# Sums of squares through PSUM on VectorE alone, and a place of its own for the last phase's scaled x, in a planned decoder-layer kernel

## The chip, the cores and the metric

The kernel runs on one core of one Trainium2 chip. The metric is the time of one execution on the device in microseconds (us); the number before is the median of three runs. The engines are named as the profile names them: PE (TensorE, matrix products; PEld is its loading of weights), DVE (VectorE), ACT (ScalarE), POOL (GpSimd) and SP (SyncE, which starts most transfers). SBUF is the working memory that all engines read and write; PSUM holds what PE produces, in eight banks, and DVE and ACT can read and write it.

## The reference

One layer of a hybrid decoder for two groups of requests: a prompt of 1024 tokens, and eight samples of one token each with a cache of 512 tokens. The width is 1024, the inner width of the two feed-forward networks 2816. Cut to what matters here:

```python
def rmsnorm(x, g):
    y = xf * lax.rsqrt(jnp.mean(xf * xf, axis=-1, keepdims=True) + NORM_EPS)
    return (y * g).astype(x.dtype)

def decoder_layer(...):
    h = x + 0.5 * rmsnorm(swiglu(rmsnorm(x, n_ffn1_pre), ffn1_gate, ffn1_up, ffn1_down), n_ffn1_post)
    u = rmsnorm(h, n_mix_pre)
    proj = u @ w_in
    ...                       # differential attention and RWKV-7 time mixing of proj
    h = h + rmsnorm(concat(ya, yb) @ w_out, n_mix_post)
    h = h + 0.5 * rmsnorm(swiglu(rmsnorm(h, n_ffn2_pre), ffn2_gate, ffn2_up, ffn2_down), n_ffn2_post)
```

So each feed-forward network has a norm in front of it and one behind it, and the mixing has one in front and one behind. Each norm needs the mean of the squares of a token's 1024 values.

## The kernel before

**Layout.** Activations lie transposed: the 1024 features are 8 tiles of 128 partitions, the tokens run along the free dimension. The tokens are cut into two halves of 512 (the eight samples ride with the first half of each feed-forward network, which makes 520), and each half into two chunks of about 260 (`CHUNKS`, line 33). The full precision of float32 is kept by splitting each operand of a large product into a high and a low part of type float32r and forming three products (`mm3`, line 678). The split of an activation is made by `pair` (line 808): ACT writes the high part with the norm's gain, DVE subtracts it again and writes the low part.

**Phases.** The trunk (`s_trunk`, line 1016) runs the feed-forward networks in four phases: ph 0 and 1 are the first network on the two halves of the tokens, ph 2 and 3 the second network. Phases 0 and 3 save products by a seven-product scheme on blocks (`seven`, `s_combine`); phase 3 builds those blocks in the SBUF region with the tag `dreg`. In between, while the trunk goes on, run the input projection (`s_project`, tiles `proj_m`), the jobs of the RWKV part (`s_job`, tiles `job_*`), attention (`s_attend`), the samples' own decode (`s_decode_a`, `s_decode_b`, tiles `dec_*` and `decb_*`), and the output projection (`s_out`, tiles `out_m` and `outb_m`).

**Where norms are formed.** `square_sum` (line 755) squares one of the 8 feature tiles on ACT and adds it to a sum; `rstd` (line 765) adds over the partitions with one matmul against a matrix of 1/1024, then takes the square root on ACT and the reciprocal on DVE. `stats` (line 799) does both for all 8 tiles of a chunk. It is called in two places:

- `s_stats` (line 1206), ahead of phases 2 and 3, with one buffer `sqs` for the squares (in the trace `stats_sqs`), the sum in the tile `bset_bv`;
- `s_tail` (line 1242), behind phases 0 and 1, for the norm ahead of the projection, with the two buffers `sq` (in the trace `tail_sq`), the sum in `init_rb` (the name `prb` in the code). The projection is run on the values without this norm, and its result is multiplied with it as it leaves PSUM (`init_E<-proj_m,init_rb`).

The sums over the down product's results (`trunk_acc` with `trunk_sq`) and over the output projection's results (`bset_la`, `bset_sg` with `init_E`) call `square_sum` directly.

With `SQP` at 0 the add goes to whichever of DVE and POOL `choose` (line 431) expects to end first. `s_pre` (line 1214) prepares x of a phase: scale with the norm, then `pair`. In phase 3 the scaled value goes into a ring of two buffers `sq` (in the trace `pre_sq`), which the block combination, the down sums and others use too; in phases 1 and 2 it overwrites its source. The split parts `pre_T` of phase 3 take the buffers that the operands of the second output projection (`outb_T`) occupied.

**Order.** Nothing is left to the order of the source. Each part is a generator of instructions, a stream, and a planner written in Python (`run`, line 478) picks at every step, for each engine, among the streams' next instructions the one with the earliest due time that can start soon. Costs come from `price` (line 380). The due times come from a backward pass over a dry run (`latest`, line 567); `PASSES` dry runs follow each other, each with the due times of the one before, and `BIAS` adds a number of microseconds to all due times of a stream (`tail1` is the second stream of the name `tail`, and so on). The chosen order is then fixed for each engine. An engine executes its own queue strictly in that order, and PE is such a queue too.

PSUM banks are handed out by name. A stream outside the trunk has one or a few: `stats`, `pre`, `lora`, `job`, `outn` and `decb` all have `dec`; a tail of phase 0 or 1 has `dec` and `aux0` in turn, where the norm of the tail's first chunk lies in `aux0` and that of its second in `aux1`. A new tile in a bank waits until the former one has been read.

Of the kernel before, what the change touches and what calls it, by code (L numbers as in the profile page):

```python
# [22 lines left out]
P = 128  # L23
# [56 lines left out]
W_DEC = 4160  # L80
# [9 lines left out]
MW = 1  # L90
MARG = 0
SLACK = 0.02
PASSES = 4
BIAS = {"trunk2": 300, "outn3": -60, "outb0": 30, "pre2": -3, "tail1": -30, "lora1": -10}
SHIFT = {}
SWAP = 0
MIX = 1
SQP = 0
RESAT = 3
GROUPS = {(0, 10): [[0, 1, 2], [3, 4], [5, 6, 7], [8, 9]], (3, 6): [[0, 1, 2], [3], [4, 5]],  # L100
          (0, 8): [[0, 1, 2], [3, 4], [5], [6, 7]], (0, 6): [[0, 1, 2], [3], [4, 5]], (3, 4): [[0, 1], [2, 3]], (3, 8): [[0, 1, 2], [3, 4], [5], [6, 7]]}
LOWS = (1, "out")
# [110 lines left out]
class Kern:  # L213
# [99 lines left out]
    def put(self, eng, op, fn, a, k):  # L313
# [14 lines left out]
        if o.late is not None:  # L328
            o.late += BIAS.get(st.part, 0) + sum(d for a, b, d in self.shift.get(st.part, ()) if a <= o.key[1] < b)
        self.price(o, op, a, k, outs[0], ins)  # L330
# [468 lines left out]
    def stats(self, src, rb, tmp=("sqs", 1), **kw):  # L799

        for k in range(KT):
            if SQP:
                self.square_sum(rb, src[k], k, self.ps2()[:, :rb.shape[-1]], engines=("vector",))
            else:
                self.square_sum(rb, src[k], k, self.tmp(*tmp, rb.shape[-1]), **kw)
        self.rstd(rb)
# [407 lines left out]
    def s_pre(self, ph):  # L1214

        half = ph % 2
        if ph > 1:
            yield ("wait", ("outw", half))
        for c, (_, n) in enumerate(CHUNKS[ph]):
            yield ("wait", ("stage", ph, c))  # L1220
            if ph:
                yield ("wait", ("stats", ph, c))
            if c == 0:
                tiles = self.two(half)
                x = self.x[ph] = self.parts(ph, *tiles)
                self.xt[ph] = [t.rearrange("p (k t) -> p k t", t=520) for t in tiles]
            for k in range(KT):
                src = self.staged[c]
                if ph:

                    t = self.tmp("sq", 2, n) if ph == 3 else src[k]
                    self.either("tensor_tensor", t, src[k], self.own[c][2][:, :n], ALU.mult)
                    src = {k: t}
                for step in self.pair(k, src, f"n_ffn{1 + ph // 2}_pre", x[c]):
                    step()
                if k % 4 == 3:
                    yield
            self.signal(("x", ph, c))
            yield
        self.signal(("staged", ph))  # L1240
# [205 lines left out]
    def s_project(self, half):  # L1446

        nc = self.nc
        places = None
        for c in range(2):  # L1450
            yield ("wait", ("prb", half, c))
        if half:
            yield ("wait", ("outw", 0))
        else:
            yield ("wait", ("loaded", 1, "up", LEAD - 1, None))
            places = ("w0", "w1"), [("used", 1, kind, LEAD - 1, None) for kind in ("gate", "up")]

        job = [16, 12, 20]
        ms = [24, 25] + job
        ms = ms + [m + i for i in range(1, 4) for m in job] + list(range(12)) if half else \  # L1460
            ms + [m + 1 for m in job] + list(range(8)) + [m + i for i in range(2, 4) for m in job] + list(range(8, 12))

        def out(i, c, ps):
            o, n = SPANS[half][c]
            po = (self.rb if i % 2 else self.E)[:, o:o + n]
            nc.vector.tensor_tensor(po, ps, self.prb[:, o:o + n], ALU.mult)
            nc.sync.dma_start(self.PT[ms[i]][:, FIRST[half] + o:FIRST[half] + o + n], po)
            if c:
                self.signal(("done", half, ms[i]))

        units = [(i, c) for i in range(len(ms)) for c in ((2,) if half and i > 1 else range(2))]
        if half:
            units[:4] = [(0, 0), (1, 0), (0, 1), (1, 1)]
        yield from self.linear(("in", half), [self.column(self.I["w_in"], m) for m in ms], units, None, out, places,
                               [(self.Li[m], half == 0) for m in ms] if "in" in LOWS else None)
        self.signal(f"proj{half}")

    def s_out(self, half):
# [1169 lines left out]
```

## Time and profile before

| what | value |
|---|---|
| runs shown | 2285.0, 2285.44 and 2281.86 us, median 2285.0 |
| the profiled execution's own time | 2287.04 us |
| its span, first to last instruction | 2284.6 us |
| granted clock of TensorE, mean | 0.995 |
| PE busy | 2223.3 us, 15857 matmuls |
| DVE, ACT, POOL busy | 1537.3, 1098.8 and 986.9 us |
| transfers | 343.15 MB, 150 GB/s in the mean |

How to read the rows that follow in the prediction. A row of a group or of a tile names the engine, the operation, what it writes and reads (`out<-in`, by the program's names), the shapes and the count; then the shortest, the median and the longest duration in ns with the first and last start in us, or the sum in us and the mean in ns, with the idle time in front. A row of the timeline begins with its start and duration in us, and what stands in brackets is the idle time of the engine before it and what ended that. A row of waits names who waited for whom, with the total in us, the count and the longest. Nearly every operation carries the line L320, since all are recorded by one helper; the tile's names tell them apart.

### The profile page before, as it was taken

What the parts mean: (1) busy time and instruction counts of PE and PEld (TensorE: products, weight loads), DVE (VectorE), ACT (ScalarE), POOL (GpSimd) and SP (SyncE); (2) the same over time, 40 slices, a digit from 0 to 9 for tenths busy, and PEclk for the clock granted to TensorE, in tenths of its full rate; (3) what the DMA queues carried; (4) which work ended last, traced back from release to release, by engine and by line L of the source; (5) the groups of instructions that cost most, each with busy time, mean ns of one, the idle gap of its engine ahead of it and who ended that gap; (6) DMA issues with size and microseconds to landing.
All of it is one profiled execution on the core that took longest, in us unless ns stands there. A gap on an engine that the chain in (4) does not pass through costs nothing.

```text
span 2284.6 us, 42790 instructions
## 1 busy us (share of the span) xinstructions
PE 2223.3 (97%) x15857; PEld 1981.1 (87%) x15857; DVE 1537.3 (67%) x3550; ACT 1098.8 (48%) x2256; POOL 986.9 (43%) x819
## 2 busy tenths in 40 slices
PE   7999999999999999999999999999999998999998
PEld 7999999799887778888877877777788888999998
DVE  5477888745766776568766466664676365778776
ACT  5443443635454366344562155543576555544444
POOL 3344555524333675456443124333434354544443
PEclk9999999999999999999999999999999999999999
DMA  6423334354433685655668753334636857434543
GB/s 203 135 84 94 110 93 131 102 148 140 113 107 104 184 244 174 211 177 151 178 205 213 193 146 111 106 86 115 199 112 172 276 165 240 148 114 126 148 139 112
DMA packets 476295, 343.15 MB, mean 150 GB/s; under 512 B 82457, under 2 KB 424061, under 8 KB 476088
## 3 DMA queue, kind: packets, MB, share of 16 engines
q1 hardware_dynamic: 475480, 338.82, 50.6%
q8 instruction: 125, 2.05, 0.4%
q0 software_dynamic: 320, 1.08, 0.1%
q14 instruction: 82, 0.67, 0.1%
q10 hardware_dynamic: 288, 0.52, 0.1%
HBM read 278.98 MB, written 61.38 MB: 149 GB/s over the span
## 4 chain that ended last, share of the span: by engine, by line
PE 77%; DVE 6%; ACT 6%; DMA 5%; issue 3%; POOL 2%; SPq 1%; DVEq 0%; ACTq 0%; POOLq 0%
PE trunk_m L320 44%; PE proj_m L320 12%; PE trunk_aux L320 7%; PE job_aux L320 4%; PE out_m L320 2%; PE outb_m L320 2%; PE attn_m L320 2%; PE attn_aux L320 1%; SPq L320 1%; ACT wts_w L320 1%; ACT mix_T L320 1%; DMA wts_raw<-in_ffn_gate_dram 1%; PE job_dec L320 1%; DMA lin_w<-Lo 1%; POOL wts_w L320 1%
## 5 line engine op out<-in xcount | busy, mean ns | idle before, releaser
L320 POOL TENSOR_TENSOR wts_w<-wts_raw,wts_w 128x1024 fp32r<-128x1024 f32 (+2 forms) x161 | 310.8, 1938 | 351.3 <-ACT wts_w L320 303.5
L320 PE MATMUL trunk_m<-trunk_xl,wts_w 128*128 128x256 f32 (+2 forms) x2700 | 456.5, 320 | 4.4 <-DVE trunk_xl L320 3.7
L320 PE MATMUL trunk_m<-pre_X,wts_w 128*128 128x512 f32 (+3 forms) x2400 | 439.9, 334 | 4.9 <-DVE pre_X L320 2.0
L320 PEld LDWEIGHTS trunk_m<-trunk_xl,wts_w 128*128 128x128 f32 x2700 | 381.4, 188 | 40.7 <-DVE trunk_xl L320 5.8
L320 PEld LDWEIGHTS trunk_m<-pre_X,wts_w 128*128 128x128 f32 x2400 | 351.3, 190 | 44.8 <-issue 3.7
L320 PE MATMUL trunk_m<-pre_T,wts_w 128*128 128x512 f32 (+3 forms) x1848 | 365.0, 348 | 6.5 <-DVE trunk_xl L320 2.7
L320 ACT CAST wts_w<-wts_raw 128x1024 fp32r<-128x1024 f32 (+2 forms) x293 | 244.2, 848 | 241.3 <-PE trunk_m L320 167.2
L320 PEld LDWEIGHTS trunk_m<-pre_T,wts_w 128*128 128x128 f32 x1848 | 288.1, 191 | 44.3 <-issue 3.9
L320 DVE TENSOR_TENSOR trunk_xl<-trunk_xl,trunk_m 128x256 f32<-128x256 f32 (+2 forms) x351 | 165.9, 491 | 57.7 <-PE trunk_m L320 56.4
L320 POOL TENSOR_TENSOR trunk_xl<-trunk_t,trunk_xl 128x512 fp32r<-128x512 f32 (+3 forms) x88 | 94.7, 1078 | 169.2 <-ACT trunk_xl L320 168.8
L320 PE MATMUL proj_m<-tail_xl,lin_w 128*128 128x256 f32 (+1 forms) x1248 | 166.5, 288 | 0.0
L320 PEld LDWEIGHTS proj_m<-tail_xl,lin_w 128*128 128x128 f32 x1248 | 153.9, 188 | 6.9 <-issue 5.1
L320 PE MATMUL proj_m<-tail_T,lin_w 128*128 128x512 f32 (+1 forms) x672 | 150.4, 380 | 3.0 <-DVE tail_T L320 1.9
L320 PEld LDWEIGHTS proj_m<-tail_T,lin_w 128*128 128x128 f32 x672 | 120.6, 188 | 31.0 <-DVE tail_T L320 3.0
L320 DVE TENSOR_TENSOR wts_w<-wts_raw,wts_w 128x1024 fp32r<-128x1024 f32 (+2 forms) x102 | 109.6, 1075 | 34.7 <-ACT wts_w L320 32.4
L320 POOL TENSOR_TENSOR lin_w<-lin_raw,lin_w 128x1024 fp32r<-128x1024 f32 x21 | 51.6, 2457 | 110.6 <-ACT lin_w L320 106.7
L320 ACT CAST wts_w<-wts_lraw 128x512 fp32r<-128x512 f32 x94 | 55.7, 619 | 72.0 <-DMA wts_lraw<-in_ffn_down_dram 35.0
L320 POOL TENSOR_TENSOR wts_w<-wts_lraw,wts_w 128x512 fp32r<-128x512 f32 x43 | 60.0, 1398 | 45.2 <-ACT wts_w L320 41.9
L320 PE MATMUL trunk_aux<-trunk_xl,wts_w 128*128 128x256 f32 (+1 forms) x516 | 71.7, 283 | 0.0
L320 DVE TENSOR_TENSOR trunk_t<-trunk_g,trunk_m 128x512 f32<-128x512 f32 (+2 forms) x75 | 41.9, 559 | 44.1 <-PE trunk_m L320 41.7
L320 PE MATMUL trunk_m<-comb_T,wts_w 128*128 128x260 f32 x540 | 69.4, 282 | 0.0
L320 ACT CAST wts_w<-wts_dec 128x512 fp32r<-128x512 f32 x30 | 17.6, 587 | 103.7 <-DVE wts_dec L320 102.0
(647 smaller groups left out, 4263.8 us busy)
## 6 DMA issues: line engine op xcount, KB each, us to landing
wts_raw<-in_ffn_gate_dram SPq DMA_DIRECT2D x88, 512.0 KB
wts_raw<-in_ffn_up_dram SPq DMA_DIRECT2D x58, 512.0 KB
wts_raw<-in_ffn_down_dram SPq DMA_DIRECT2D x56, 384.0 KB
wts_raw<-in_ffn_down_dram SPq DMA_DIRECT2D x29, 512.0 KB
lin_raw<-in_w_in_dram SPq DMA_DIRECT2D x26, 512.0 KB
wts_w<-Ld SPq DMA_DIRECT2D x22, 512.0 KB
mix_T<-PT SPq DMA_DIRECT2D x37, 256.0 KB
Ld<-wts_w SPq DMA_DIRECT2D x24, 384.0 KB
```

Source lines behind the costliest of these rows:

```text
L320: o = Op(eng, lambda: fn(*a, **k), st)
```

## The change

Three things are edited, beside one switch without effect (`ODD = 0` leaves the line in `s_project` as it was).

1. `SQP` names the two kinds of buffers for which `stats` now puts the square of each feature tile into a PSUM bank of the stream (`ps2`) instead of an SBUF buffer, and gives the add to DVE alone. Both callers of `stats` are named, so it holds for the norms ahead of phases 2 and 3 (from the bank `dec`) and for those behind phases 0 and 1 (from `dec` and `aux0` in turn). The sums over the down product and over the output projection keep their SBUF buffers and their choice of engine.
2. In phase 3 `s_pre` takes the region `dreg` as a place for all 16 scaled tiles of x, where it had the ring of two buffers `sq`.
3. The planner makes three passes instead of four, and other streams have other biases.

```diff
-PASSES = 4
-BIAS = {"trunk2": 300, "outn3": -60, "outb0": 30, "pre2": -3, "tail1": -30, "lora1": -10}
+PASSES = 3
+BIAS = {"trunk2": 300, "outn3": -50, "outb0": 90, "pre2": -3, "prep1": 3, "job11": 3, "job12": 30, "states0": -3, "lora0": 10, "lin1": -3, "stats0": -30, "mix0": -30, "stats2": -60, "decb0": 30, "attn01": -3, "stats1": 30, "fin0": -60}
...
-SQP = 0
+SQP = ("sqs", "sq")
+ODD = 0
...
     def stats(self, src, rb, tmp=("sqs", 1), **kw):
         for k in range(KT):
-            if SQP:
+            if SQP and tmp[0] in SQP:
                 self.square_sum(rb, src[k], k, self.ps2()[:, :rb.shape[-1]], engines=("vector",))
             else:
                 self.square_sum(rb, src[k], k, self.tmp(*tmp, rb.shape[-1]), **kw)
...
+                scaled = self.T(self.pool, [P, W_DEC], "dreg") if ph == 3 else None
             for k in range(KT):
                 src = self.staged[c]
                 if ph:
-                    t = self.tmp("sq", 2, n) if ph == 3 else src[k]
+                    t = scaled[:, 2112 * c + n * k:2112 * c + n * k + n] if ph == 3 else src[k]
                     self.either("tensor_tensor", t, src[k], self.own[c][2][:, :n], ALU.mult)
...
-                               [(self.Li[m], half == 0) for m in ms] if "in" in LOWS else None)
+                               [(self.Li[m], half == 0) if not ODD or m % 2 else () for m in ms] if "in" in LOWS else None)
```

## The prediction

> **What bounds the kernel now.** First I read the top of the page, for the engine that is never free.
>
> ```profile
> span 2284.6 us, 42790 instructions
> PE 2223.3 (97%) x15857; PEld 1981.1 (87%) x15857; DVE 1537.3 (67%) x3550; ACT 1098.8 (48%) x2256; POOL 986.9 (43%) x819
> ```
>
> TensorE (PE) is busy for 2223.3 of 2284.6 us, and the change touches no matmul of the weights. So all that can be won or lost is PE's idle time, 61.3 us, plus what a lower granted clock adds after a pause. Next I read the table of stages, to see where that idle time lies. Its columns are the stretch, its length, then PE, PEld, DVE, ACT and POOL busy, then the granted clock and the DMA share.
>
> ```profile
> 0.00:40.00 40.00, 28.21 (x175) 25.88 (x176) 21.36 (x56) 22.98 (x44) 15.30 (x17) 0.91 0.46 136
> 395.00:460.00 65.00, 59.84 (x323) 51.22 (x322) 45.73 (x77) 39.30 (x72) 35.56 (x39) 0.95 0.33 100
> 540.00:1000.00 460.00, 454.34 (x3336) 386.26 (x3336) 311.43 (x881) 219.37 (x498) 216.25 (x156) 1.00 0.53 158
> 1000.00:1120.00 120.00, 119.81 (x626) 101.62 (x625) 97.38 (x190) 51.84 (x85) 70.27 (x56) 1.00 0.55 162
> 1120.00:1190.00 70.00, 63.77 (x394) 56.48 (x394) 53.72 (x94) 45.29 (x80) 33.94 (x39) 0.98 0.72 217
> 1146.00:1160.00 14.00, 10.41 (x68) 9.61 (x66) 10.13 (x22) 9.87 (x18) 6.64 (x10) 0.88 0.18 51
> 1320.00:1770.00 450.00, 439.05 (x2936) 347.61 (x2935) 290.96 (x838) 251.19 (x587) 169.18 (x111) 1.00 0.47 132
> 1770.00:1905.00 135.00, 128.97 (x862) 116.36 (x861) 68.34 (x114) 74.53 (x133) 56.90 (x61) 1.00 0.68 210
> 1905.00:1960.00 55.00, 51.04 (x412) 50.63 (x411) 31.59 (x63) 32.86 (x63) 25.55 (x33) 0.97 0.91 278
> 2260.00:2284.60 24.60, 16.69 (x141) 15.81 (x139) 13.68 (x29) 15.11 (x36) 10.42 (x14) 0.95 0.23 87
> ```
>
> Length minus PE busy is the idle time: 11.8 us at the start and 7.9 us at the end, which no edit here reaches; 5.2 us around the tail of phase 0 (395 to 460); 6.2 us around the tail of phase 1 (1120 to 1190); 10.0 us around the hand-over to the last phase (6.0 and 4.0); and 5.7 and 11.0 us in the two stretches of jobs and attention. The moved norms lie at the tails (ph 0 and 1) and ahead of phases 2 and 3.
>
> **The change part by part.** *Part 1, squares to PSUM, sums on DVE.* There are four norms of two chunks with seven added squares each, 56 adds. These rows say who does them now.
>
> ```profile
> L320 POOL TENSOR_TENSOR init_rb<-init_rb,tail_sq x23: 737/754/1666, 427.4 to 1178.8; 128x256 f32<-128x256 f32 x16, 128x264 f32<-128x264 f32 x7
> L320 DVE TENSOR_TENSOR init_rb<-init_rb,tail_sq x5: 411/425/427, 438.1 to 1178.2; 128x256 f32<-128x256 f32 x5
> L320 DVE TENSOR_TENSOR bset_bv<-bset_bv,stats_sqs x16: 410/431/2385, 1011.9 to 1875.5; 128x256 f32<-128x256 f32 x12, 128x264 f32<-128x264 f32 x4
> L320 POOL TENSOR_TENSOR bset_bv<-bset_bv,stats_sqs x12: 734/770/1729, 1015.3 to 1873.1; 128x256 f32<-128x256 f32 x9, 128x264 f32<-128x264 f32 x3
> L320 DVE TENSOR_TENSOR trunk_xl<-trunk_xl,trunk_m 128x256 f32<-128x256 f32 x142 | 58.4, 414 | 14.5 <-PE trunk_m L320 14.1
> L320 ACT ACTIVATE job_dec<-mix_T,setup_rmu 128x512 f32<-128x512 f32 x24 | 16.6, 690 | 24.0 <-DMA mix_T<-PT 9.5 <-DVE job_stf L320 5.3 <-issue 3.5
> L320 ACT ACTIVATE mix_T<-mix_T,setup_cols 128x512 f32<-128x512 f32 x8 | 5.7, 716 | 0.0
> ```
>
> POOL does 23 + 12 = 35 adds at about 0.76 us and loses 27 us of work; DVE gains 35 adds. A DVE add with one operand in PSUM is in the trace (trunk_xl, 414 ns), so DVE gains at least 35 x 0.414 = 14.5 us over the whole span, at 67% busy. A Square of ScalarE (ACT) written to PSUM is not in the trace. Its bounds come from the two scaling activations of 512 columns: 690 ns into PSUM against 716 ns into SBUF, so between 0 and 26 ns less for each; I take 0, since for 56 squares even the other end is 1.5 us on an engine with half its time free.
>
> What matters is what the POOL adds do to their neighbours, and the tail of phase 1 shows it.
>
> ```profile
> L320 DVE SCALAR_TENSOR_TENSOR tail_T<-trunk_xl,setup_cols,tail_T x8: 474/904/955, 1140.0 to 1144.6; 128x256 fp32r<-128x256 f32 x8
> L320 DVE SCALAR_TENSOR_TENSOR trunk_xl<-trunk_xl,setup_cols,tail_aux x16: 468/476/481, 1132.7 to 1159.0; 128x256 f32<-128x256 f32 x16
> 1142.73 3.46 POOL L320 TENSOR_TENSOR init_rb<-init_rb,tail_sq 128x256 f32<-128x256 f32 x4 [1.24 <-ACT tail_sq L320]
> PE proj_m L320 <- DVE tail_T L320: 1.9, 5, 0.9
> PE tail_aux L320 <- DVE trunk_acc L320: 1.7, 1, 1.7
> PE proj_m L320 <- ACT tail_T L320: 1.1, 1, 1.1
> PE decb_dec L320 <- ACT init_rb L320: 0.9, 1, 0.9
> ```
>
> The eight low halves (tail_T, two inputs in SBUF) have a median of 904 ns while POOL adds squares; the same operation with its second tensor in PSUM (tail_aux) keeps to 476 ns. PE waits 1.9 us for these low halves. If POOL's adds are gone and DVE does the halves ahead of its own adds, 0.48 us apiece keeps pace, and I take the whole 1.9 us. The other two waits hang on the order in ACT and POOL, where chunk 0's squares, at 3.46 / 4 = 0.87 us a step, stand ahead of chunk 1's: tail_aux 1.7 and decb_dec 0.9 us. I take half, 1.3 us (bounds 0 and 2.6). The 1.1 us for ACT's high halves, released by POOL's residual adds, stay. The clock of 0.88 over 14 us costs 14 x 0.12 = 1.7 us; with half of the pauses there gone I take 0.8 (bounds 0 and 1.7). **Sum at this tail: -4.0 us**, bounds 0 and -6.2, and +2.9 if the adds go ahead of the halves (below).
>
> The Trainium skill ("SBUF — State Buffer", Who interferes with whom) calls this an exclusive lock, held for a whole instruction, between DVE with two SBUF inputs and a GpSimd operation that reads SBUF. By that rule a half of 0.48 us behind a POOL add of 0.74 us would take 1.22 us, and eight of them would win 5.9 us of DVE time. The trace's 0.904 us is less than the rule's, and by it eight win 8 x 0.43 = 3.4 us.
>
> At the tail of phase 0 the same adds are hidden.
>
> ```profile
> 420.95 24.06 PE L320 MATMUL trunk_m<-pre_T,wts_w 128*128 128x512 f32 x96 [1.99 <-DVE wts_w L320]
> 448.71 1.75 DVE L320 RECIPROCAL init_rb<-init_rb 128x256 f32<-128x256 f32 x1 [1.20 <-ACT init_rb L320]
> 449.00 0.30 PEld L320 LDWEIGHTS tail_aux<-init_rb,init_onesD 128*128 128x128 f32 x2 [0.52 <-POOL init_rb L320]
> 459.78 0.42 DVE L320 TENSOR_TENSOR init_E<-proj_m,init_rb 128x256 f32<-128x256 f32 x1 [1.90 <-PE proj_m L320]
> ```
>
> PE runs weights of phase 1 through from 421 to 445, chunk 0's norm is ready at 450.5, and its reader at 459.78 was waiting for PE. The pauses of this stage lie earlier, at 395 to 421, in the down sums and the weights. **0 us**, bounds -0.5 and 0. The norm ahead of phase 2 stands in 1000 to 1120, where PE idles 0.2 us in 120 over the matmuls of phase 1: **0 us**.
>
> *Part 2, own place for the scaled x of phase 3.* It removes the two-slot ring pre_sq and adds no instruction, DMA or queue; its region (dreg) is free until the block combination, which waits for the whole of x anyway.
>
> ```profile
> 1851.27 0.92 ACT L320 ACTIVATE pre_T<-pre_sq,setup_cols 128x264 fp32r<-128x264 f32 x2 [1.90 <-PE outb_m L320]
> 1852.46 1.67 POOL L320 TENSOR_TENSOR pre_sq<-outb_T,bset_bv 128x264 f32<-128x264 f32 x2 [2.28 <-DVE pre_T L320]
> 1890.40 0.49 DVE L320 SCALAR_TENSOR_TENSOR pre_T<-pre_sq,setup_cols,pre_T 128x256 fp32r<-128x256 f32 x1 [0.30 <-ACT pre_T L320]
> 1908.01 6.09 PE L320 MATMUL trunk_m<-pre_T,wts_w 128*128 128x264 f32 x48 [1.88 <-ACT trunk_sq L320]
> ```
>
> Now POOL makes two columns, then waits for pre_T (2.28 us), which itself had to wait for the output projection to leave that buffer. With 16 places POOL can finish chunk 0 before 1851. But x of phase 3 is complete at 1890.9 and first read at 1908.0: 17 us of cover, so its being earlier is worth nothing in itself. What is worth something is that six scale-and-split steps, and part of part 1's adds, leave the crowded stretch of 1860 to 1908. The waits there that ACT, POOL and DVE end are these.
>
> ```profile
> PE rows_cb L320 <- ACT rows_X L320: 2.2, 2, 1.5
> PE trunk_m L320 <- ACT trunk_sq L320: 1.9, 1, 1.9
> PE trunk_m L320 <- POOL wts_w L320: 1.0, 2, 0.6
> PE trunk_m L320 <- DVE trunk_xl L320: 0.8, 1, 0.8
> ```
>
> Together 5.9 us. Most hang on the order at a busy engine, not on the sum of work; I take a third, **-2.0 us** (bounds -5.9 and 0).
>
> *Part 3, the planner.* One pass less and other biases (microseconds on due times) renew the order of every queue; ODD at 0 changes nothing. No operation is added. The pauses exposed to it, 5.7 + 11.0 = 16.7 us, are chains of small matmuls with copies between. No row prices a new order; the bounds are -16.7 (every pause closed) and +16.7 (all doubled). I take **-1.0 us**, near the zero that an order as dense as now would give.
>
> **Sum**: -4.0 - 2.0 - 1.0 = -7.0 us. The profiled execution took 2287.04 us, its span 2284.6 plus 2.4 outside; the median of the shown runs is 2285.0, 2.0 less, and I carry the difference to it: **2278 us**.
>
> **The rivals.** (1) *Hidden anyway, or given back.* The planner puts DVE's add between every two low halves: 0.48 + 0.42 = 0.90 us, the pitch of today (904 ns), and the relief of part 2 falls into the 17 us of cover. For it: DVE is the fuller engine at that tail, 53.7 of 70 us against POOL's 33.9. Then -2 us remains at most: 2283.
>
> (2) *Slower: DVE's queue at the tails.* If the sums stand ahead of the halves and of the down sums (trunk_xl), then PE waits 7 x 0.414 = 2.9 us for each of four chunks, 11.6 us: 2297. It decides from the point where an add is issued before a low half while PE has no other ready matmul. Against it: the norm is needed only when the projection leaves PSUM, later than its operands.
>
> (3) *A worse order, or a bank that blocks.* Chunk squares now borrow the PSUM bank "dec", which the decode's RWKV step uses at the same tail; the wait decb_dec for ACT init_rb (0.9 us) is that bank already. Four squares in it, each 0.41 + 0.42 us with their reader, are 3.3 us a visit; with two visits, and half of the 16.7 us of pauses added, 2285 + 6.7 + 8.3 - 4 = 2296.
>
> The Trainium skill ("PSUM — Partial Sum Buffer", PSUM bank collisions raise a hardware error) speaks against the change here: two engines may not be in one bank at a time, so software must guard it. By that rule the squares through one bank go one after the other; no run here shows it yet for squares.
>
> (4) *A clearly better order*, half of the 16.7 us closed besides the forecast: 2270.
>
> **How the numbers follow.** A measurement of this kernel tells about 0.2%, 4.6 us, from no change: 2280.4 to 2289.6. Forecast, with its own range of 2272 to 2281, 0.38; rival 4, 0.18; rival 1, 0.22; rival 2, 0.09; rival 3, 0.13. Faster is the forecast and rival 4, 0.56; the same 0.22; slower 0.22. The range takes in most of rivals 2 and 3, and below the full bound of the tail and the hand-over with half of the order's (6.2 + 5.9 + 8.3 = 20.4): 2264 to 2297.
>
> **What would show it.** Right: no POOL adds into init_rb and bset_bv; tail_T at about 0.48 us and PE's wait for it under 0.5 us in the tail of phase 1; that stage with under 3 us idle; pre_sq (under its new tile name) done for chunk 0 before the projection ends; the stretches of jobs within 3 us of now. Wrong: tail_T still at 0.9 us pitch, PE waiting for DVE init_rb or on a dec bank, x of phase 3 complete after trunk 2's last matmul, or idle time in 540 to 1000 or 1320 to 1770 changed by more than the tails.

## The result and the profile after

The changed kernel takes 2286.95 us (median of 19 runs) against 2283.8 us of the kernel before (19 runs on the same chip): a ratio of 1.002, 95% interval 1.0012 to 1.0028. One of its 19 runs took 6021 us and is left out of the ratio. It is slower by 3 us between the medians and by 0.2%, some 4.6 us, in the ratio, where 7 us less had been forecast. The profiled execution after took 2288.53 us, its span is 2286.8 us; the one before took 2287.04 us, 3 to 5 us above the medians that the kernel before shows beside the experiments (2282.0 to 2283.8). So the two profiles serve to find places, and the totals come from the ratios.

First the head of the page after and its table of stages (stretch, length, busy time of PE, PEld, DVE, ACT and POOL, granted clock, DMA).

```profile
PE 2228.5 (97%) x15857; PEld 1980.8 (87%) x15857; DVE 1540.9 (67%) x3575; ACT 1091.6 (48%) x2246; POOL 994.3 (43%) x804
```

```profile
395.00:460.00 65.00, 64.01 (x387) 56.65 (x388) 44.41 (x85) 41.08 (x73) 41.56 (x37) 1.00 0.35 106
540.00:1000.00 460.00, 454.36 (x3274) 381.76 (x3272) 306.47 (x828) 220.51 (x504) 201.24 (x148) 1.00 0.53 153
1000.00:1120.00 120.00, 114.09 (x565) 94.85 (x565) 93.74 (x208) 47.72 (x76) 58.83 (x48) 0.97 0.55 164
1120.00:1190.00 70.00, 66.93 (x447) 60.33 (x447) 50.07 (x98) 43.94 (x82) 47.38 (x40) 1.00 0.73 221
1905.00:1960.00 55.00, 50.86 (x393) 50.10 (x394) 33.11 (x70) 31.38 (x61) 25.56 (x34) 0.91 0.85 266
```

The idle time did not go, it moved. The tail of phase 0 (395 to 460) fell from 5.2 us of idle time to 1.0, the tail of phase 1 (1120 to 1190) from 6.2 to 3.1; but 1000 to 1120 had 0.2 us and now has 5.9, and the clock at the hand-over (1905 to 1960) fell from 0.97 to 0.91. POOL is busier than before (994.3 against 986.9 us) although it adds none of the 56 squares any more: the planner gave it other work.

A second reading says where the time goes, without fixed stretches. I add up the columns of all matmuls in the order in which they start, and take for each kernel the time at which it reaches the sum that the kernel before had at a given time. The difference is PE's progress; a negative change in a stretch is time won there (us, one profile of each).

```
before's time      0-540  540-1000  1000-1120  1120-1200  1200-1860  1860-1960   sum
after               -8.4      +4.3      +11.4       -7.7       -0.3       +3.0  +2.1
both_old_plan       +2.4      -3.1       +9.5       -6.6       +4.9       +8.6 +15.4
plan_only           -8.4     +10.9       +6.5      +11.6       +6.7      +19.1 +46.3
squares_old_plan    +1.2      -0.9       +5.7       -6.9       +5.4      +13.4 +17.6
place_old_plan      -1.3      +0.0       +0.0       +0.9       -0.1       +3.5  +3.0
squares_new_plan    -8.7      +3.3      +10.2       -8.2       -0.1      +18.6 +14.9
frozen_squares      -0.7      +0.1       +0.0       +2.7       -4.1       -1.7  -3.9
frozen_place        +1.1      -0.2       +0.0       +2.1       -0.2       +0.8  +3.5
frozen_both         +0.5      +5.4       +0.0       +2.2       -1.7       +0.5  +6.7
frozen_sbuf         -2.4      -1.9       +0.2       -0.3       -3.5       -2.0 -10.1
splice500           -7.9      -1.0       -0.1       +0.1       -1.1       -1.7 -11.6
splice_mixed        -7.6      -0.4       +0.2       -0.3       -1.8       -2.3 -12.2
```

(The sum includes the rest up to the end, 0.3 us at most.) frozen_place has the instructions of the kernel before in the same order up to 1850 us and still differs by 2.1 us in one stretch, and frozen_both by 5.4 us in one where PE gets the same instructions (last section). So a stretch is read only together with a wait that stands in it. The first row is the result in one line: 8 us won at the tail of phase 0, where I had put nothing; 4 and 11 us lost in two places where I had put nothing; 8 us won at the tail of phase 1, where I had put 4; and 3 lost at the hand-over, where I had put a gain of 2. The 4.3 us from 540 to 1000 have no wait behind them: PE is idle 5.6 us there and was idle 5.7 before, and frozen_both loses 5.4 us there in the order of before. So they are not shown to be the new order's.

The changed squares themselves look as forecast, or better. The rows of the tiles after (shortest, median, longest duration in ns):

```profile
L321 ACT ACTIVATE tail_dec<-trunk_xl x7: 362/389/390, 1158.7 to 1168.9; 128x256 f32<-128x256 f32 x7
L321 DVE TENSOR_TENSOR bset_bv<-bset_bv,stats_dec x28: 351/414/431, 997.7 to 1895.9; 128x256 f32<-128x256 f32 x21, 128x264 f32<-128x264 f32 x7
```

An add of DVE took up to 2.4 us before (row in the prediction); these never take more than 0.43 us. So the cost must come from what stands around the adds.

### The profile page after: what moved, and what is told of

Same layout as the page of the kernel before. It is cut to its first block, busy times and chain, and to the rows that moved or that the text cites. A ratio compares the mean times of both kernels' runs of the same rounds, so it can differ in the third digit from the quotient of the medians.

```text
span 2286.8 us, 42822 instructions
## 1 busy us (share of the span) xinstructions
PE 2228.5 (97%) x15857; PEld 1980.8 (87%) x15857; DVE 1540.9 (67%) x3575; ACT 1091.6 (48%) x2246; POOL 994.3 (43%) x804
## 4 chain that ended last, share of the span: by engine, by line
PE 78%; DVE 7%; ACT 5%; DMA 4%; issue 3%; POOL 2%; SPq 1%; DVEq 0%; ACTq 0%; POOLq 0%
PE trunk_m L321 46%; PE proj_m L321 11%; PE trunk_aux L321 7%; PE job_aux L321 5%; PE out_m L321 2%; PE attn_m L321 2%; PE attn_aux L321 1%; PE outb_m L321 1%; POOL wts_w L321 1%; DMA lin_w<-Lo 1%; ACT wts_w L321 1%; PE job_dec L321 1%; SPq L321 1%; PE job_cb L321 1%; DVE trunk_xl L321 1%
## 5 line engine op out<-in xcount | busy, mean ns | idle before, releaser
L321 POOL TENSOR_TENSOR wts_w<-wts_raw,wts_w 128x1024 fp32r<-128x1024 f32 (+2 forms) x169 | 335.5, 1991 | 438.2 <-ACT wts_w L321 329.3
L321 DVE TENSOR_TENSOR wts_w<-wts_raw,wts_w 128x1024 fp32r<-128x1024 f32 (+2 forms) x94 | 101.1, 1075 | 33.6 <-ACT wts_w L321 33.2
```

Of the source, the lines that this page charges most:

```text
L321: o = Op(eng, lambda: fn(*a, **k), st)
```

## Experiments: one part of the change at a time, planned anew

The theory at first (A) was that the new biases give back what the sums on DVE win; its rivals that DVE's extra work gives it back (B), or that every new order is a draw of some 5 us (C). Three edits switch the parts. The planner runs as it does in the kernels.

```diff
 both_old_plan, squares_old_plan, place_old_plan: the biases of before
-PASSES = 3
+PASSES = 4
-BIAS = {"trunk2": 300, "outn3": -50, "outb0": 90, ...}
+BIAS = {"trunk2": 300, "outn3": -60, "outb0": 30, "pre2": -3, "tail1": -30, "lora1": -10}
 place_old_plan, plan_only: squares in SBUF, added by DVE or POOL
-SQP = ("sqs", "sq")
+SQP = 0
 squares_old_plan, plan_only, squares_new_plan: the ring of two
-                    t = scaled[:, 2112 * c + n * k:2112 * c + n * k + n] if ph == 3 else src[k]
+                    t = self.tmp("sq", 2, n) if ph == 3 else src[k]
```

> Both edits of the work (squares through PSUM added by DVE, own place for the scaled x of phase 3), but planned with the passes and biases of the kernel before. Theory A, the plan gives it back: the sums on DVE win about 8 us at the tail of phase 0 and about 7 us at the tail of phase 1, and what is lost at 1001 us (PE waits 5.0 us for DVE wts_w) and at 1905 to 1940 us comes from the new biases; then this kernel is faster than before by 8 to 15 us, 2269 to 2276 us, and has no wait for DVE wts_w over 1 us around 1000 us. Theory B, the work gives it back: DVE's 35 more adds make it late for the weights' low halves under any plan; then 2280 to 2290 us with a pause of 3 to 6 us ahead of phase 2's norm. Theory C, every new order is a draw of some 5 us to either side, without regard to the edits: 2279 to 2289 us, pauses at places that have nothing to do with the norms.

> The kernel before with nothing but the new passes and biases; squares stay in SBUF, POOL may add them, the scaled x keeps its ring of two. Theory A: the biases by themselves lose, since the late output projection and the early norm of phase 2 stay and nothing is won at the tails: 2288 to 2300 us. Theory B: the biases are harmless, 2279 to 2287 us. Theory C: anything from 2279 to 2289 us.

> The kernel before with only the squares through PSUM and their sums on DVE; old passes and biases, old ring of two for the scaled x. Theory A: faster by 8 to 15 us, 2269 to 2276 us, with both tails shortened (PE's progress 6 to 9 us ahead after the tail of phase 0, and again 5 to 8 us won at the tail of phase 1). Theory B: 2280 to 2290 us, with pauses for DVE wts_w or DVE trunk_g of 3 to 6 us more. Theory C: 2279 to 2289 us.

> The kernel before with only the own place for the scaled x of phase 3; old passes and biases, squares in SBUF and added by DVE or POOL. Theories A and B: 2281 to 2285 us, for the 17 us between the last column of x and its first reader hide it, and nothing ahead of 1850 us moves by more than 2 us. Theory C: 2279 to 2289 us, with differences also ahead of 1850 us, where the edit does nothing.

> The changed kernel (new passes and biases) without the own place: the scaled x of phase 3 is back in its ring of two; planned anew. Theory D: nothing changes ahead of 1850 us; at the hand-over the order is another draw, so 2279 to 2295 us, with the difference all between 1850 and 1960 us. Were the own place a gain of 2 us as forecast, this is about 2289 us; were it the cause of POOL's 6.55 us run of scalings ahead of the adds that PE waits for, it is 2281 to 2284 us.

| work | old passes and biases | new passes and biases |
|---|---|---|
| before's | 1 (2282.1 us) | plan_only 1.0209 (1.0196 to 1.0222), 2329.9 us |
| squares alone | squares_old_plan 1.0126 (1.0111 to 1.0140), 2309.9 us | squares_new_plan 1.0072 (1.0059 to 1.0085), 2299.3 us |
| place alone | place_old_plan 1.0011 (1.0001 to 1.0022), 2285.5 us | not run |
| both | both_old_plan 1.0114 (1.0097 to 1.0132), 2306.2 us | the changed kernel 1.002 (1.0012 to 1.0028) |

(Theory D in the last of the five expectations is the one of the next section; it was run with that section's kernels.)

All three theories fail, C by its size; squares_new_plan, at 2299.3 us, also lies above all that was expected of it. The edits of the work alone cost 1.1%, the planner's numbers alone 2.1%, and together 0.2%: the two parts do not add up. The same edit, the squares, costs 1.3% with the old numbers. With the new ones it stands between 1.0209 and 1.0072: it saves 1.3%. The own place costs 0.11% (0.01 to 0.22) beside the old numbers and saves 0.5% beside the new ones (1.0072 to 1.002). The passes were not tried apart from the biases. The lead at the tail of phase 0 belongs to the new numbers, for plan_only has it with the old work (-8.4 us) and the kernels with old numbers do not. The gain at the tail of phase 1 comes with the squares, under both sets of numbers (-6.9, -6.6, -8.2, -7.7). And each of these kernels loses at the hand-over, most where a sum is late for PE. The longest wait of PE there, in plan_only:

```profile
PE trunk_m L320 <- DVE trunk_xl L320: 16.1, 2, 15.6
```

One wait of 15.6 us for a down sum: in the table 19.1 of its 46.3 us lie in this one stretch.

## Experiments: the order held still

To price the edits without a new order, the kernel was made to write down, in a dry run of the kernel before, which instruction each queue takes in which place and which engine each free choice takes, and then to follow that record with the changed work. An instruction that isn't ready in its place is taken as soon as it is.

```diff
+        if self.replay:                      # choose()
+            return self.engines[key] if self.engines[key] in engines else engines[0]
...
+            if self.replay:                  # run(): the earliest of the record among those ready
+                o = min(c, key=lambda o: self.picks[o.key])
...
+    build(plans[-1][2], True)                # records picks and engines
+    Kern.replay = True                       # then SQP and the place of x are switched
     nc = build(plans[-1][2], False)
```

> The order of every queue is that of the kernel before, written down in a dry run of it and then followed; only the work differs: the squares of the norms go to PSUM, and each add that POOL did stands at the same place of the order on DVE. Theory D, the order was fitted to the old costs: the edit itself is worth what it does to its neighbours, 0 to 6 us less with the gain at the tail of phase 1, and the 28 us that the same edit lost under the old passes and biases came from the renewed order; 2277 to 2284 us. Theory E, DVE's 35 more adds are too many at the norms under any order: 2288 to 2310 us, with PE waiting for DVE trunk_xl by 4 us or more ahead of the last phase.

> The order of the kernel before, followed as written down; only the scaled x of phase 3 gets its own place. Theory D: POOL and DVE can only start earlier, never later than before, so 2280 to 2284 us, and the 5.5 us that PE waits at the last norm when the same edit is planned anew do not show. Theory E, the place itself costs (POOL runs its scalings in a row and takes the shared access from DVE): 2285 to 2290 us.

> Both edits of the work in the order of the kernel before. Theory D: the sum of the two single ones, 2275 to 2284 us. Theory E: 2288 to 2310 us.

Squares 1.0014 (1.0004 to 1.0024), place 1.0009 (1.0000 to 1.0019), both 1.0026 (1.0015 to 1.0037). Theory D is right that most of the loss under the old numbers was the order's (28 us against 3), and wrong that the edits win: they lose a little, and with both, at 2289.34 us, the time is in the range that theory E gave. The timeline at the tail of phase 1 tells why. First the kernel before: DVE makes eight low halves while POOL adds, then PE sums (tail_dec) and DVE takes the reciprocal.

```profile
1140.05 5.54 DVE L320 SCALAR_TENSOR_TENSOR tail_T<-trunk_xl,setup_cols,tail_T 128x256 fp32r<-128x256 f32 x8
1147.56 0.43 DVE L320 TENSOR_TENSOR init_rb<-init_rb,tail_sq 128x256 f32<-128x256 f32 x1 [0.92 <-POOL init_rb L320]
1150.26 1.75 DVE L320 RECIPROCAL init_rb<-init_rb 128x256 f32<-128x256 f32 x1 [2.27 <-ACT init_rb L320]
```

Then frozen_squares, DVE and PE:

```profile
1140.28 4.10 DVE L323 SCALAR_TENSOR_TENSOR tail_T<-trunk_xl,setup_cols,tail_T 128x256 fp32r<-128x256 f32 x8
1144.30 0.41 DVE L323 TENSOR_TENSOR init_rb<-init_rb,tail_dec 128x256 f32<-128x256 f32 x1
...
1149.54 0.42 DVE L323 TENSOR_TENSOR init_rb<-init_rb,tail_dec 128x256 f32<-128x256 f32 x1 [0.45 <-ACT tail_dec L323]
1151.97 1.75 DVE L323 RECIPROCAL init_rb<-init_rb 128x256 f32<-128x256 f32 x1 [2.01 <-ACT init_rb L323]
```

```profile
1142.06 5.13 PE L323 MATMUL proj_m<-tail_T,lin_w 128*128 128x256 f32 x39 [0.25 <-DVE tail_T L323]
1150.11 0.67 PE L323 MATMUL tail_dec<-init_rb,init_onesD 128*128 128x256 f32 x2 [2.92 <-DVE init_rb L323]
```

The low halves do what I forecast: eight in 4.10 us, where they took 5.54 and POOL's adds held them up, and PE then runs 39 matmuls without a stop. But the sum that follows is late. Chunk 0's squares have one bank (`dec`; chunk 1 has `aux0`), and each square waits until DVE has read the one before: (1149.54 - 1144.30) / 6 = 0.873 us a step. POOL's adds had run beside the low halves; now they stand behind them. PE waits 2.92 us, and the reciprocal comes at 1151.97 instead of 1150.26.

The Trainium skill ("PSUM — Partial Sum Buffer", PSUM bank collisions raise a hardware error) has software keep two engines out of one bank at a time. The trace agrees, an add of 0.42 us and then 0.45 us until the next square is there, one after the other; but it does not test the rule, since each square also overwrites the one before and so has to wait for its reader.

> The order of the kernel before; the squares stay in SBUF with their rings, and DVE alone adds them at the places that the adds have in that order. Against the same order with squares through PSUM this leaves out the one bank that a square and its add take in turns. Theory H, the bank sets the pace (0.875 us a square at the tail of phase 1, PE waits 2.9 us for the sum): here ACT runs a square ahead, the pace is 0.45 to 0.5 us, PE's wait for the sum at that tail is under 1 us, and the time 2279 to 2283 us. Rival I, what costs is that POOL no longer adds while DVE makes the low halves: the wait stays at 2 to 3 us and the time at 2284 to 2287 us.

The edit puts the squares back into their SBUF buffers and leaves the adds with DVE alone:

```diff
-                self.square_sum(rb, src[k], k, self.ps2()[:, :rb.shape[-1]], engines=("vector",))
+                self.square_sum(rb, src[k], k, self.tmp(*tmp, rb.shape[-1]), engines=("vector",))
```

The ratio is 0.9995 (0.9986 to 1.0004), 2279.94 us: theory H. DVE at the same place in frozen_sbuf, and then PE's wait:

```profile
1139.85 3.59 DVE L323 TENSOR_TENSOR init_rb<-init_rb,tail_sq 128x256 f32<-128x256 f32 x7
```

```profile
PE tail_dec L323 <- DVE init_rb L323: 0.8, 1, 0.8
```

Seven adds take 3.59 us, 0.51 each, and the wait is 0.8 us. So it is the single bank that costs in this order, 0.14 + 0.05 = 0.19% or 4 us, and not DVE's load. (The SBUF buffers at the tails are two, the bank is one; a second bank was not tried.)

## Experiments: where the changed kernel's own order loses

The place at 1001 us first. DVE and then PE in the changed kernel:

```profile
991.33 1.76 DVE L321 RECIPROCAL outn_aux<-bset_la 128x256 f32<-128x256 f32 x1 [11.76 <-ACT bset_la L321]
...
994.61 3.15 DVE L321 SCALAR_TENSOR_TENSOR out_T<-out_T,setup_cols,outn_aux 128x256 f32<-128x256 f32 x8
997.67 0.41 DVE L321 TENSOR_TENSOR bset_bv<-bset_bv,stats_dec 128x256 f32<-128x256 f32 x1
...
1004.25 0.42 DVE L321 TENSOR_TENSOR bset_bv<-bset_bv,stats_dec 128x256 f32<-128x256 f32 x1 [0.44 <-ACT stats_dec L321]
1004.58 1.80 DVE L321 TENSOR_TENSOR wts_w<-wts_raw,wts_w 128x1024 fp32r<-128x1024 f32 x1
```

```profile
1006.44 0.80 PE L321 MATMUL trunk_m<-pre_T,wts_w 128*128 128x512 f32 x1 [5.02 <-DVE wts_w L321]
```

Six of the seven adds of chunk 0 stand ahead of a weight's low half, and PE needs that half. In the kernel before this norm's adds begin at 1011.9 us (row in the prediction). The next edits move places in the recorded order (their lines are shortened here).

```diff
 low_first: places in the record of the changed kernel
+    for key, rank in [((("wts", 0), 546), 10139.5), ((("wts", 0), 549), 10177.5)]:
+        Kern.picks[key] = rank
 low_first_x_later: also
+    for n in range(30, 48): Kern.picks[("pre", 3), n] = 17795 + n / 100
 norm_later: with low_first's
+    for n in range(15, 36): Kern.picks[("stats", 0), n] += 45.5
```

> The changed kernel in its own order, with two instructions of DVE moved up: the low halves of the weights that PE waits for at 1001 us stand ahead of the adds of phase 2's norm instead of between the sixth and the seventh. Theory J, that place in DVE's queue is the cause of the 5.0 us wait and of the 4 us of lower clock behind it: 6 to 9 us less than the changed kernel, 2278 to 2281 us. Rival K, the 9 us are a hole that only moves (the weights are then ready, and PE waits for what DVE did instead): 2284 to 2288 us.

> The same, and at the hand-over to the last phase the last six scale-and-split steps of x of phase 3 (own place, chunk 1) stand behind the sums of squares that PE waits for 4.2 us there. Theory J: a further 3 to 7 us less, 2272 to 2277 us. Rival L, x itself is then late for the last phase: a wait for DVE pre_T of 2 to 6 us ahead of its first matmuls, and no gain over the kernel with the first move alone.

> The changed kernel in its own order, with DVE's two low halves moved up as in low_first and the rest of phase 2's norm (the matmul that sums chunk 0, and what follows it) put some 13 groups of the trunk's matmuls later. Theory M, the 9 us lost from 1000 to 1020 us are the norm's: its matmul stands in PE's queue ahead of the trunk's while DVE still has eight column scalings and seven adds to do; then the wait for DVE bset_bv (5.6 us in low_first) and the clock behind it go, PE's progress loses under 3 us there in place of 10, and the time is 2280 to 2285 us. Rival N, DVE is simply full there and another wait of 4 us or more takes the place: 2287 to 2292 us.

Ratios to before: low_first 1.0049 (1.0037 to 1.0061), low_first_x_later 1.0046 (1.0034 to 1.0059), norm_later 1.0023 (1.0014 to 1.0032); none is faster than the changed kernel's 1.002. The holes only move (rivals K and N; low_first, at 2291.63 us, is even above K's range). PE's wait in low_first, its waits from 995 to 1030 us in norm_later, and one wait of low_first_x_later:

```profile
1007.96 1.22 PE L323 MATMUL stats_dec<-bset_bv,init_onesD 128*128 128x256 f32 x2 [5.57 <-DVE bset_bv L323]
```

```profile
PE trunk_m L323 <- ACT wts_w L323: 2.1, 1, 2.1
PE stats_dec L323 <- DVE bset_bv L323: 1.4, 1, 1.4
PE trunk_m L323 <- DVE trunk_g L323: 1.2, 1, 1.2
PE trunk_m L323 <- POOL wts_w L323: 0.8, 1, 0.8
```

```profile
PE trunk_m L323 <- DVE trunk_xl L323: 12.1, 11, 6.6
```

With the low half early PE waits for the norm's sum, 5.57 us; with the norm later it waits 5.5 us in four pieces. Counted in columns the stretch 1000 to 1120 loses 11.4, 12.3 and 11.3 us in the changed kernel, low_first and norm_later. So no single instruction is the cause. At 991 us DVE, which had waited 11.76 us for ACT bset_la, gets the scalings of the output projection, the new norm and two weights at once, and the order has nothing else for PE. Which bias makes this pile (`stats0` at -30 is the nearest) was not tried. At the hand-over the 4.2 us wait for POOL is gone in low_first_x_later, and one of 6.6 us for a down sum of DVE stands in its place, at 1915 us and ahead of the last phase's first matmuls: no gain, as rival L had it, though it is not x that is late.

> The work of the changed kernel, both edits, in its own order up to some 1820 us of the span, and in the order of the kernel before from there on. Theory O, the 5 us that the changed kernel loses at the hand-over to the last phase are its order's, not the edits': 2279 to 2284 us, PE's progress at 1960 us about 4 us ahead of the changed kernel's. Rival P, the own place or the sums on DVE cost that much there in any order: 2285 to 2289 us.

1.0113 (1.0094 to 1.0132), 2307.8 us, and neither O nor P: the two orders do not meet at the seam. 19.5 us are lost between 1200 and 1860 us, all of them behind 1830 us, and 2.4 from 1860 to 1960. This run tells nothing about the hand-over.

> The changed kernel, its own order kept, with its squares back in SBUF and their rings (two places at the tails, one ahead of phases 2 and 3); DVE alone adds them, and x of phase 3 keeps its own place. If the bank that a square and its add take in turns costs in this order too (4 us between frozen_squares and frozen_sbuf), 2281 to 2285 us. If the new order, which was made with the squares in PSUM, leaves room for the turns, as the changed kernel's 1.5 us of waits at the tail of phase 1 suggest, 2285 to 2289 us. Slower than the changed kernel if the ring of one and DVE's reads from SBUF next to POOL cost more: 2290 us or more.

1.0122 (1.0106 to 1.0138), 2311.1 us: 1% or some 24 us above the changed kernel with the same order, as the last of the three expectations has it (2290 us or more), by far more than was expected. The adds in after_sbuf:

```profile
L323 DVE TENSOR_TENSOR bset_bv<-bset_bv,stats_sqs x28: 355/530/2021, 1003.5 to 1917.5; 128x256 f32<-128x256 f32 x21, 128x264 f32<-128x264 f32 x7
L323 DVE TENSOR_TENSOR init_rb<-init_rb,tail_sq x28: 409/426/2512, 432.6 to 1212.3; 128x256 f32<-128x256 f32 x21, 128x264 f32<-128x264 f32 x7
```

In the new order POOL works beside the adds: 18 of the 56 take over 0.7 us, each of them while an operation of POOL runs in the trace, and these 18 hold 17 us above 0.42 us each. Of the other 38, 16 overlap POOL as well and stay short. So the same edit, squares from SBUF to PSUM, costs 0.19% in the old order and saves 1% in the new. How much of the 24 us are the long adds, and how much is an order followed with work that it was not made for, was not separated.

## Experiments: what is worth keeping

The lead at the tail of phase 0 first, in the rows of the two 15 us stretches there, the kernel before and then after:

```profile
395.00:410.00 15.00, 11.90 (x85) 10.94 (x84) 10.88 (x26) 8.15 (x17) 6.53 (x9) 0.94 0.16 45
410.00:425.00 15.00, 13.01 (x77) 11.63 (x77) 13.83 (x25) 11.12 (x21) 12.48 (x16) 0.84 0.48 158
```

```profile
395.00:410.00 15.00, 14.29 (x113) 13.81 (x114) 11.55 (x29) 8.09 (x16) 6.71 (x9) 1.00 0.01 1
410.00:425.00 15.00, 14.71 (x78) 12.27 (x77) 10.03 (x20) 9.86 (x16) 14.72 (x15) 1.00 0.45 141
```

Idle time falls by (14.29 + 14.71) - (11.90 + 13.01) = 4.1 us, and the clock is worth 15 x (0.06 + 0.16) = 3.3 us more: 7.4 us. The clock's part is the chance of one execution. frozen_squares has the old order here, with waits of 2.23 and 1.98 us for PE in the same two places, and its clock stays at 1.00:

```profile
395.00:410.00 15.00, 10.66 (x79) 9.46 (x77) 11.70 (x26) 8.10 (x14) 6.77 (x9) 1.00 0.01 1
410.00:425.00 15.00, 12.99 (x80) 11.02 (x79) 14.33 (x25) 12.36 (x27) 10.07 (x13) 1.00 0.54 178
```

Against it the lead is (14.29 + 14.71) - (10.66 + 12.99) = 5.4 us, all of it idle time. After, the weights' low halves in this stretch are POOL's and none is DVE's:

```profile
L321 POOL TENSOR_TENSOR wts_w<-wts_raw,wts_w x3: 2408/2409/2417, 412.1 to 421.6; 128x1024 fp32r<-128x1024 f32 x3
```

Before, DVE made one, among the tail's scalings:

```profile
L320 DVE TENSOR_TENSOR wts_w<-wts_raw,wts_w x1: 1219/1219/1219, 419.7 to 419.7; 128x1024 fp32r<-128x1024 f32 x1
```

PE waited 1.99 us for it (row in the prediction).

splice500 takes the new numbers' order up to 500 us and the old one from there, with the work of before; splice_sbuf and splice_mixed add DVE-only sums from SBUF.

```diff
+    Kern.picks = {k: first.get(k, 1e6 + i) for k, i in Kern.picks.items()}   # first: new order, below 500 us
 splice_mixed: as before at the tail of phase 0
-            if SQP and tmp[0] in SQP:
+            if SQP and tmp[0] in SQP and self.cur.part not in ("tail0", "tail1"):
```

> The work of the kernel before (squares in SBUF, POOL may add them, ring of two). Its order follows the new passes and biases up to 500 us, through the tail of phase 0, and the order of the kernel before from there on. Theory F, the 8 us that the changed kernel is ahead after the tail of phase 0 are the new order's alone, and nothing later takes them back unless its own order does: 2274 to 2278 us. Rival G, the lead at the tail of phase 0 is work pulled forward, which leaves a hole later: 2281 to 2285 us, with the lead of PE's progress gone by 1000 us.

> The order of splice500 (new order through the tail of phase 0, then the old one) with the squares in SBUF and DVE alone adding them, as in frozen_sbuf; old ring of two for the scaled x. If the two add up (0.17 and 0.05% less than before) it is 2275 to 2278 us; if the order of the tail of phase 0 has already taken what DVE's adds can win, it is as splice500, 2276 to 2279 us. A version faster than both kernels either way, unless the new order's tail needs POOL's adds: then 2281 us or more.

> The order of splice500. The squares of the tail of phase 0 as in the kernel before (POOL and DVE add them); those of the tail of phase 1 and of the norms ahead of phases 2 and 3 in SBUF with DVE alone adding. splice_sbuf lost 5.5 us at the tail of phase 0, where PE waited 2.2 us for DVE's sum; if that is all that it lost, this is 2274 to 2277 us, as fast as splice500 or 1 us faster. If DVE's adds cost in the later stages as well, 2278 to 2281 us.

splice500: 0.9983 (0.9973 to 0.9992), 2276.5 us, theory F. Its lead of 7.9 us at 540 us stays to the end; the medians give 5.5 us, as the reading against frozen_squares does. splice_sbuf: 1.0004 (0.9994 to 1.0014); PE waits at the tail of phase 0 for DVE's sum:

```profile
PE tail_dec L323 <- DVE init_rb L323: 2.2, 1, 2.2
```

In this order POOL's adds are needed there. splice_mixed leaves them to POOL and takes DVE alone for the later norms: 0.9973 (0.9962 to 0.9984), 2276.5 us. It beats both kernels; over splice500 it is not shown to be faster (the intervals overlap).

## Why the prediction was wrong

- **The step that failed is part 3, "I take -1.0 us, near the zero that an order as dense as now would give", and with it the sum, which adds the three parts as if each had a size of its own.** A new order is no such term. In the changed kernel it won 8.4 us (5.4 without the chance of the clock) at the tail of phase 0 and lost 11.4 from 1000 to 1120. With the old work the same numbers cost 2.1%, about 48 us, outside my bound of 16.7. Parts 1 and 2, -6.0 us in the sum, cost 0.26% or 6 us when the order is held still. From there to the changed kernel's 0.2% it is -1.4 us, less than the two intervals tell apart. So by that path part 3 looks met; that is luck, what is left of gains and losses of 5 to 11 us.
- **Part 1 at the tail of phase 1, -4.0 us: the stage won more (-7.7), and not for my reason.** In a fixed order the low halves sped up as I said and PE still lost 2.2 and 2.7 us (both edits, squares alone), since the squares through one bank take turns. That was a rival's mechanism (3): I had 3.3 us for four squares, 0.83 us each; it is 0.873. (Rival 2 has 2.9 us of waiting for each chunk, and PE waits 2.92 us here; that is luck, for the adds do not stand ahead of the halves.) Planned anew with the squares in PSUM, the tail won 7 to 8 us in all four kernels; why was not separated. Its low halves are no faster there: over both chunks the median was 688 ns before and is 712 ns in the changed kernel, so the sign that I named, 0.48 us, fails while the stage still wins.

```profile
L320 DVE SCALAR_TENSOR_TENSOR tail_T<-trunk_xl,setup_cols,tail_T x16: 471/688/962, 1140.0 to 1167.9; 128x256 fp32r<-128x256 f32 x16
L321 DVE SCALAR_TENSOR_TENSOR tail_T<-trunk_xl,setup_cols,tail_T x16: 469/712/1987, 1156.9 to 1178.5; 128x256 fp32r<-128x256 f32 x16
```

- **"0 us" at the tail of phase 0 and "0 us" for the norm ahead of phase 2** held for the edits in the old order (frozen_squares -0.7 and 0.0 us) and not in the new one. I had argued from covers in the old order, and the order was one of the things that changed.
- **Part 2, -2.0 us, failed.** In the old order the place costs 0.09% (0.00 to 0.19), planned anew with old numbers 0.11%. At the hand-over PE waits for another sum in nearly every order, with the ring and without it. In the changed kernel POOL, DVE and PE there read:

```profile
1899.69 6.55 POOL L321 TENSOR_TENSOR pre_dreg<-outb_T,bset_bv 128x256 f32<-128x256 f32 x8 [4.56 <-DVE bset_bv L321]
1906.21 1.77 POOL L321 TENSOR_TENSOR trunk_acc<-trunk_acc,trunk_sq 128x256 f32<-128x256 f32 x2
```

```profile
1904.19 4.06 DVE L321 SCALAR_TENSOR_TENSOR pre_T<-pre_dreg,setup_cols,pre_T 128x256 fp32r<-128x256 f32 x5 [0.26 <-ACT pre_T L321]
```

```profile
1908.03 1.22 PE L321 MATMUL last_aux<-trunk_acc,init_onesD 128*128 128x256 f32 x2 [4.16 <-POOL trunk_acc L321]
...
1912.38 7.97 PE L321 MATMUL trunk_m<-pre_T,wts_w 128*128 128x264 f32 x48 [1.11 <-ACT wts_w L321]
```

  POOL makes eight scalings in a row, ahead of the two adds that PE waits for. That the own place brings this about is not shown: with the ring and the same numbers (squares_new_plan) the stretch loses 18.6 us in place of 3.0. The 17 us of cover of x had shrunk to 4: it was complete at 1908 us and first read at 1912.4.
- **The rivals.** Slower came about, by neither rival's sum. Rival 3's first half (the bank) and second half (a worse order) were both at work, for less than its 11 us, while the new order won 8 us elsewhere. (Two visits of 3.3 us are 6.6, not 6.7; its 2296 stays.)

## What to carry to other kernels

When a planner lays out every queue, price an edit with the order held still (record it, follow it with the new work) and price the order by itself: here the squares alone were +0.14%, planned anew +1.3%, and the planner's numbers alone +2.1%. If an edit must be planned anew, look first at the few places where PE's queue meets the end of another stream's chain, for there lie the longest waits of these kernels. Handing a chain of producer and consumer a single PSUM bank makes it take turns; leave it in SBUF where the other engine is idle (a second bank was not tried).

## What the runs showed of the hardware that was not expected

- The length of a short pause does not settle whether the clock falls. Before, two waits of 2.24 us (below) and 1.99 us went with a granted clock of 0.84 from 410 to 425 us; in frozen_squares waits of 2.23 and 1.98 us left it at 1.00, and the same 23 matmuls took 2.96 us in place of 4.47. Of the six profiles that have these two waits, three show the loss (before, frozen_place, frozen_both) and three do not (frozen_squares, frozen_sbuf, place_old_plan). Before, then frozen_squares:

```profile
407.79 4.47 PE L320 MATMUL trunk_m<-pre_T,wts_w 128*128 128x256 f32 x23 [2.24 <-DVE trunk_xl L320]
```

```profile
405.38 2.96 PE L323 MATMUL trunk_m<-pre_T,wts_w 128*128 128x256 f32 x23 [2.23 <-DVE trunk_xl L323]
```

- Waits of 4 to 5 us went with a lower clock in both places of the changed kernel, around 1001 and 1906 us:

```profile
1000.00:1020.00 20.00, 14.27 (x49) 11.21 (x50) 16.40 (x32) 11.69 (x22) 15.51 (x19) 0.83 0.73 220
1900.00:1920.00 20.00, 14.46 (x85) 13.46 (x86) 15.44 (x26) 11.38 (x22) 13.24 (x17) 0.74 0.58 185
```

  5.7 us idle with 20 x 0.17 = 3.4 us of clock, and 5.5 us idle with 20 x 0.26 = 5.2 us. These are at most what the clock cost, since it can be low during the pause itself.

- The clock can fall without a pause. From 575 to 595 us PE has the same instructions in the kernel before and in frozen_both, many of them small matmuls of the RWKV part, and no wait is longer than 0.7 us. Before, then frozen_both:

```profile
575.00:585.00 10.00, 9.51 (x167) 7.74 (x162) 4.19 (x8) 4.98 (x11) 0.10 (x1) 1.00 0.60 166
```

```profile
575.00:585.00 10.00, 9.27 (x107) 7.19 (x108) 4.19 (x7) 2.53 (x6) 0.10 (x1) 0.62 0.47 118
585.00:595.00 10.00, 9.57 (x130) 7.86 (x130) 3.04 (x11) 3.83 (x9) 0.00 (x0) 0.87 0.19 55
```

  10 x (0.38 + 0.13) = 5.1 us of the 5.4 that this profile is behind there. What decides it was not tried; it bounds what one execution can show.
- A Square of 256 columns from ACT takes 389 ns into PSUM; before, into SBUF, 414 ns. The gain of 25 ns lies at the top of my bounds of 0 and 26, and it changed nothing.

```profile
L320 ACT ACTIVATE tail_sq<-trunk_xl x14: 400/414/422, 1142.3 to 1175.2; 128x256 f32<-128x256 f32 x14
```
